# An encoder layer on one core: operands of wide products moved to byte 480 of a line of 512, and work beside the recurrence ordered anew

## The chip, the cores and the metric

The kernel runs on one core of a Trainium2 chip. Its time is the device time of one execution in microseconds (us). Engines are called as the profile calls them: PE (TensorE, with PEld for its weight loads), DVE (VectorE), ACT (ScalarE), POOL (GpSimd) and SP (SyncE, which issues the transfers). SBUF has 128 partitions; a tile lies at the same byte of each, and "byte 480 of a line of 512" means that this address, modulo 512, is 480.

## The reference

One layer of a bidirectional encoder, on two groups of 512 tokens with a model width of 1024 and shared weights, all in fp32:

```python
x = LN(alpha*x + 0.5*SwiGLU_1(x))                       # D_FF = 2816
h = x @ W_in                                            # MLA, RWKV-7 and gate columns
A = MLA(h_q, h_kv) @ P_mla                              # 8 heads
B = RWKV7_bidir(h_rwkv) @ P_rwkv                        # 8 heads of 64, both directions
x = LN(alpha*x + (sig(g_A)*A + sig(g_B)*B) @ W_o)
x = LN(alpha*x + CrossAttn(x, LN(mem)))                 # 4 heads of 128, 256 memory rows
x = LN(alpha*x + 0.5*SwiGLU_2(x))
```

The RWKV-7 part is a recurrence over the tokens: a state S of 64 x 64 per head is updated as S = S*w + (S a) b^T + v k^T and read as S r, once forward and once backward.

## The kernel before, in words

**Products.** Every fp32 matrix product is made of three products of rounded parts: high by high, high by low, low by high (`Bank.prod`, line 228; `Bank.mm` issues each at line 215). A "wide" product is one such matmul of 128 x 128 weights (the stationary operand) by 128 x 512 values (the moving operand). The weights are `whl` (high and low half in one tile); the moving operands are `xh` and `xl` (high and low parts of the activations, class `Acts`), `xo` (a streamed operand of a Strassen product, both parts in one tile), `mh` and `ml` (memory), `kp`, `cx`, `wd`, `ad`, `lw` and others in the projections and in MLA. There are 9344 of them with 512 columns.

**Weights.** `Stream.fetch` (line 136) has SP load a tile `wraw` of 128 x 1024, ACT cast it to the high half of `whl` (line 245), and an engine named by `Stream.low` subtract it for the low half (a "split", line 246 where that is POOL, 179 where it is DVE). `Stream.ahead` says how many tiles ahead of use this is done.

**Stages, in order of time.** FFN 1 (8 to 690 us) and FFN 2 (2056 to 2732) run as Strassen products of seven (`ffn`, `strassen`): a gate/up part (50 to 430 and 2056 to 2470), in which blocks of 36 products of `xh` and `xl` alternate with blocks of 48 of `xo`, and a down part (430 to 650 and 2470 to 2700) on `xo` alone. Between them: projections and MLA (690 to 1222), the recurrence (1222 to 1762), the last projections, W_o and cross attention (to 2055).

**The recurrence** (class `Recurrence`) handles four pairs of heads, called heads 0 to 3, one after another: `front` (products `bk` by `ar`), `inverse`, `chunks`. `inverse` inverts 32 x 32 triangular blocks: a loop of 30 steps on DVE (products `tm<-lw,dw`, then `dw<-dw,lw`, then `dw<-dw,tm`), transposes of `dw` to `xt` and `ct`, then 2 x 64 small matmuls, first of `xt` by `phi`, copied to `qt`, then of `ct` by `qt`, copied to `phi` (the "section"). `chunks` carries the state through eight chunks (`gs`, `uv`, `sn`). In the recurrence `Stream.low` is POOL and `Stream.ahead` 1.

**Work beside it.** A generator (`gate_work`, `memory_work`, `mla_work`) yields steps that do not depend on the recurrence. One step is one k-block: three wide products. `Recurrence.fill` takes steps at the place where it is called in the program, and the table `FILL` says how many each head takes in its front, in its loop (spread over 30 steps) and in its chunks.

**Order.** The program is written in one sequence, and a scheduler lists the instructions of each engine by it and by the waits between them. From the first product of `xt` on, and through the chunks, PE's order is pinned to the written one (`k.in_order`); `order` (line 195) adds such a dependency between two instructions of one engine without a wait.

**Addresses.** Pools on the left side of SBUF are stacked upward in the order in which they are opened, and pools on the right side downward from the top. Tiles of the right side (`whl`, some of the `Acts`) begin at byte 480 of a line of 512, since the top lies there; those of the left side begin wherever the sizes before them lead.

Of the kernel before, what the change touches and what calls it, by code (L numbers as in the profile page):

```python
# [11 lines left out]
F32 = mybir.dt.float32  # L12
# [45 lines left out]
PAUSE = 8  # L58
A_FILL = A_END - 16

FILL = ((72, 66, 30), (6, 50, 36), (8, 54, 36), (0, 38, 20))
STREAM_B = (
    tiles_of("w_ck", range(4), 8)
    + [("w_cv", k, n) for k in range(8) for n in range(4)]
# [713 lines left out]
def kernel(  # L778
# [79 lines left out]
    )  # L858


    rs = ExitStack()
    wp = ctx.enter_context(pool("w", "right"))
    x0 = ctx.enter_context(ExitStack())
# [52 lines left out]


    bp = ExitStack()
    bon = bp.enter_context(pool("bonus")).tile([P, HP, NC, G], F32, name="bon")
    with pool("p2") as sb:  # L920

        def tmp(tag, bufs):
# [170 lines left out]
        with pool("mla") as sm:  # L1093
# [8 lines left out]
            for h in range(HP):  # L1102
# [3 lines left out]
                for g in range(G):  # L1106
                    ks = shifted(proj(w, g), 3 + 3 * h)
                    b = aux()
                    b.prod(b.t, [((lw[0:64, 0, cols], lw[0:64, 1, cols]), (ad[0:64, 0, g], ad[0:64, 1, g]))])
                    ta = tmp("ta", 2)  # L1110
                    nc.scalar.activation(out=ta, in_=b.t, func=AF.Tanh, scale=0.5, bias=ha0[:, h : h + 1])
                    sq = tmp("sq", 2)
                    nc.scalar.activation(out=sq, in_=ks, func=AF.Square, scale=v("k_k", h))
                    b = Bank(k, "b")
                    for i in range(4):
                        b.mm(b.t[:, 2 * i : 2 * i + 2], sq[:, i * P : i * P + P], blk2)
                    m = sb.tile([P, 8], F32, name="kkn", tag="kkn", bufs=2)
                    nc.vector.tensor_scalar(out=m, in0=b.t[:, 0:8], scalar1=1e-24, scalar2=None, op0=ALU.max)
                    rstd_of(k, sb, m, "kk")
                    b = Bank(k, "b")  # L1120
                    mw = tmp("u", 1)
                    nc.vector.tensor_copy(mw.rearrange("p (a v) -> p a v", v=C), m.unsqueeze(2).to_broadcast([P, 8, C]))
                    for i in range(4):
                        b.tr(b.t[:, i * P : i * P + P], mw[:, i * P : i * P + P], k.ident)
                    nr = tmp("nr", 2)
                    nc.vector.scalar_tensor_tensor(
                        out=nr, in0=ks, scalar=nkk_c[:, h : h + 1], in1=b.t, op0=ALU.mult, op1=ALU.mult)
                    nc.sync.dma_start(out=d_rw[h][g][:, 1], in_=nr)
                    u = tmp("u", 1)
                    nc.gpsimd.tensor_scalar(  # L1130
                        out=u, in0=ta, scalar1=-1.0, scalar2=hka[:, h : h + 1], op0=ALU.add, op1=ALU.mult)
                    kn = tmp("kn", 2)
                    nc.vector.scalar_tensor_tensor(out=kn, in0=u, scalar=1.0, in1=ks, op0=ALU.add, op1=ALU.mult)
                    nc.sync.dma_start(out=d_rw[h][g][:, 3], in_=kn)
                    nc.gpsimd.tensor_scalar(out=ta, in0=ta, scalar1=-0.5, scalar2=-0.5, op0=ALU.mult, op1=ALU.add)
                    nc.gpsimd.tensor_tensor(out=ta, in0=ta, in1=nr, op=ALU.mult)
                    nc.sync.dma_start(out=d_rw[h][g][:, 2], in_=ta)
                    kp.append(kn)
                    attend(3)
# [86 lines left out]
    with pool("rw") as sb:  # L1226
# [4 lines left out]
        def early_rows():  # L1231
# [3 lines left out]
            for g in range(G):  # L1235
                ys.append(Acts(xpools[0], "x", 4, HP, "y"))
                rows(ys[g], [d_y[h][g] for h in range(HP - 1)])

        rec.memory = memory_norm(k, sb, mem, d_mt)
        for h, beside in enumerate(FILL):  # L1240
            rec.front(h, beside[0])
# [315 lines left out]
class Recurrence:  # L1557
# [106 lines left out]
    def inverse(self, h, beside):  # L1664
# [17 lines left out]
        dw = t4("dw")  # L1682
        nc.scalar.copy(dw, lw)
        lm, dm = lw.rearrange("p (i k) -> p i k", k=32), dw.rearrange("p (i k) -> p i k", k=32)
        for i in range(1, 31):
            if i < 30:
                tm = self.sb.tile([P, 256], F32, name="tm", tag="tm", bufs=2)
# [11 lines left out]
            if i < 30:  # L1699
                o = dm[:, i + 2 : 32, 0:i]  # L1700
                nc.vector.tensor_tensor(out=o, in0=o, in1=t, op=ALU.add)
        nc.vector.memset(dw[:, 0:1024:33], 1.0)
        xt, ct = t4("xt"), t4("ct")
        nc.vector.transpose(out=tj(xt), in_=dw.rearrange("p (t s) -> p s t", s=32))
# [3 lines left out]
        ra, rb = ([slice(64 * e + o, 64 * e + o + 32) for e in range(2)] for o in (0, 32))  # L1708

        k.in_order, k.pe_last = True, None  # L1710
        for j0, tag in ((0, "c"), (16, "b")):
            ps = [self.bank(tag) for _ in range(2)]
            for j in range(16):
                for e in range(2):
                    ps[e].mm(ps[e].t[rb[e], j * 32 : j * 32 + 32], phi[ra[e], e, j0 + j, 32:64], xt[ra[e], j0 + j])
            for e, cp in ((0, nc.scalar.copy), (1, nc.vector.tensor_copy)):
                cp(qt[rb[e], j0 : j0 + 16], ps[e].t[rb[e]].rearrange("p (j s) -> p j s", s=32))
        for j in (0, 16):
            for q in range(4):
                (nc.scalar.copy if q % 2 else nc.vector.tensor_copy)(diag(q, j), ct[32 * q : 32 * q + 32, j : j + 16])  # L1720
        for j0, tag in ((0, "c"), (16, "b")):
            ps = [self.bank(tag) for _ in range(2)]
            for j in range(16):
                for e in range(2):
                    ps[e].mm(ps[e].t[ra[e], j * 32 : j * 32 + 32], qt[rb[e], j0 + j], ct[rb[e], j0 + j])
            for e, cp in ((0, nc.scalar.copy), (1, nc.vector.tensor_copy)):
                cp(phi[ra[e], e, j0 : j0 + 16, 32:64], ps[e].t[ra[e]].rearrange("p (j s) -> p j s", s=32))
        k.in_order = False

    def chunks(self, h, beside, early_rows):  # L1730
# [260 lines left out]
```

## Time and profile before

| what | value |
|---|---|
| time, three runs | 2731.43, 2730.34, 2730.81 us; median 2730.81 |
| the profiled execution's own time | 2733.67 us |
| its span on the core | 2731.9 us |
| mean granted clock of PE | 0.968 |

PE is the busiest engine over the whole span. The page's second part shows the granted clock in 40 slices:

```profile
PE   8999999999999999997988887999999999999996
DVE  7888887999476888748474758656888888887987
PEclk9999999999999999998989898999999999999998
```

Each digit is a busy share in tenths, 9 being 90% or more, and for PEclk the clock that the throttle granted; a slice is 2731.9/40 = 68.3 us. Rows of windows give the start and end of the window and its length in us, then busy time and count of PE, PEld, DVE, ACT and POOL, the granted clock, the share of the DMA engines and GB/s. Rows of groups give line, engine, operation, output and inputs, shape and count, then busy us and the mean ns of one instruction, then the idle time before them and what ended it. Since matmuls are pipelined, the mean duration of one is longer than the distance from one start to the next; where PE has no idle, the distance is window length by count. Rows of the timeline give start and length in us. Rows of waits give the wait in all, how often, and the longest.

### The profile page before, as it was taken

What the parts mean: (1) busy time and instruction counts of PE and PEld (TensorE: products, weight loads), DVE (VectorE), ACT (ScalarE), POOL (GpSimd) and SP (SyncE); (2) the same over time, 40 slices, a digit from 0 to 9 for tenths busy, and PEclk for the clock granted to TensorE, in tenths of its full rate; (3) what the DMA queues carried; (4) which work ended last, traced back from release to release, by engine and by line L of the source; (5) the groups of instructions that cost most, each with busy time, mean ns of one, the idle gap of its engine ahead of it and who ended that gap; (6) DMA issues with size and microseconds to landing.
All of it is one profiled execution on the core that took longest, in us unless ns stands there. A gap on an engine that the chain in (4) does not pass through costs nothing. (4 is left out here: it accounts for less than half of the span.)

```text
span 2731.9 us, 40963 instructions
## 1 busy us (share of the span) xinstructions
PE 2576.3 (94%) x15344; PEld 2067.5 (76%) x15344; DVE 2098.0 (77%) x3742; ACT 1073.5 (39%) x1972; POOL 682.5 (25%) x465
## 2 busy tenths in 40 slices
PE   8999999999999999997988887999999999999996
PEld 7888887787767777776777666777787888887784
DVE  7888887999476888748474758656888888887987
ACT  5344332222453554554433432223544443342222
POOL 0233332442200001132123221102012323232443
PEclk9999999999999999998989898999999999999998
DMA  4344437671254433353434354451202443447751
GB/s 174 123 155 162 147 134 301 237 264 60 99 175 155 124 107 116 111 172 121 120 100 132 109 166 127 144 181 44 65 16 81 166 147 139 143 171 271 275 201 66
DMA packets 167143, 396.06 MB, mean 145 GB/s; under 512 B 41952, under 2 KB 52448, under 8 KB 166944
## 3 DMA queue, kind: packets, MB, share of 16 engines
q1 hardware_dynamic: 166944, 393.43, 41.8%
q8 instruction: 122, 2.00, 0.3%
q14 instruction: 77, 0.63, 0.1%
HBM read 259.41 MB, written 133.96 MB: 144 GB/s over the span
## 5 line engine op out<-in xcount | busy, mean ns | idle before, releaser
L215 PE MATMUL ps<-xo,whl 128*128 128x512 f32 x3792 | 896.9, 395 | 14.8 <-DVE z L179 9.1
L215 PE MATMUL ps<-xh,whl 128*128 128x512 f32 x2688 | 888.6, 402 | 15.3 <-ACT xh L245 12.9
L215 PEld LDWEIGHTS ps<-xo,whl 128*128 128x128 f32 x3792 | 712.9, 189 | 183.9 <-DVE z L179 6.9
L215 PEld LDWEIGHTS ps<-xh,whl 128*128 128x128 f32 x2688 | 509.3, 191 | 128.4 <-ACT xh L245 13.5
L215 PE MATMUL ps<-xl,whl 128*128 128x512 f32 x1344 | 536.2, 399 | 1.4 <-POOL xl L246 1.2
L245 ACT CAST whl<-wraw 128x512 fp32r<-128x512 f32 (+4 forms) x314 | 220.2, 712 | 296.3 <-PE ps L215 273.8
L179 DVE TENSOR_TENSOR whl<-wraw,whl 128x512 fp32r<-128x512 f32 (+4 forms) x269 | 277.4, 1042 | 59.5 <-ACT whl L245 59.2
L215 PEld LDWEIGHTS ps<-xl,whl 128*128 128x128 f32 x1344 | 256.4, 191 | 55.7 <-POOL xl L246 3.7
L684 POOL TENSOR_TENSOR s<-s,up 128x512 f32<-128x512 f32 x80 | 117.2, 1465 | 615.7 <-DVE up L179 394.8
L245 ACT CAST whl<-wt 128x512 fp32r<-128x512 f32 (+3 forms) x280 | 148.9, 557 | 270.3 <-PE ps L215 162.3
L179 DVE TENSOR_TENSOR whl<-wt,whl 128x512 fp32r<-128x512 f32 (+3 forms) x280 | 214.8, 788 | 13.5 <-ACT whl L245 13.5
L246 POOL TENSOR_TENSOR whl<-wraw,whl 128x1024 fp32r<-128x1024 f32 x45 | 108.8, 2419 | 364.8 <-ACT whl L245 321.3
L245 ACT CAST hop<-s 128x512 fp32r<-128x512 f32 x128 | 79.7, 623 | 244.7 <-POOL s L684 183.3
L179 DVE SCALAR_TENSOR_TENSOR x<-ps,x 128x512 f32<-128x512 f32 x184 | 124.6, 683 | 60.8 <-PE ps L215 57.1
L179 DVE TENSOR_TENSOR hop<-s,hop 128x512 fp32r<-128x512 f32 x128 | 121.1, 947 | 59.9 <-ACT hop L245 52.1
L246 POOL TENSOR_TENSOR xl<-x,xh 128x512 fp32r<-128x512 f32 x48 | 67.0, 1428 | 303.4 <-ACT xh L245 288.3
L179 DVE TENSOR_TENSOR wt<-wraw 128x512 f32<-128x512 f32 (+3 forms) x140 | 110.0, 787 | 1.3 <-DMA wraw<-in_wf_dram 0.2
L179 DVE TENSOR_TENSOR wt<-wraw,wt 128x512 f32<-128x512 f32 (+3 forms) x140 | 102.1, 730 | 5.5 <-DMA wraw<-in_wf_dram 3.5
L582 POOL TENSOR_TENSOR x<-x,s 128x512 f32<-128x512 f32 x48 | 70.2, 1467 | 129.0 <-DVE x L179 129.0
L179 DVE TENSOR_TENSOR p<-ps,p 128x512 f32<-128x512 f32 x120 | 82.3, 686 | 5.1 <-PE ps L215 1.5
L582 POOL TENSOR_TENSOR x<-x,z 128x512 f32<-128x512 f32 x48 | 71.2, 1484 | 52.7 <-DVE x L179 47.5
L215 PE MATMUL ps<-mh,whl 128*128 128x512 f32 x256 | 82.1, 398 | 1.0 <-ACT whl L245 1.0
(308 smaller groups left out, 3647.0 us busy)
## 6 DMA issues: line engine op xcount, KB each, us to landing
d_h<-hop SPq DMA_DIRECT2D x140, 512.0 KB, 2.6
xo<-d_h SPq DMA_DIRECT2D x140, 512.0 KB, 7.0
wraw<-in_wf_dram SPq DMA_DIRECT2D x95, 512.0 KB, 3.5
wraw<-in_wa_dram SPq DMA_DIRECT2D x57, 512.0 KB, 3.7
wraw<-in_wb_dram SPq DMA_DIRECT2D x32, 512.0 KB, 3.7
wraw<-in_wf_dram SPq DMA_DIRECT2D x36, 384.0 KB, 3.8
ld<-d_rw SPq DMA_DIRECT2D x24, 512.0 KB, 4.6
d_gate<-t SPq DMA_DIRECT2D x32, 256.0 KB, 2.3
```

The source lines that it names most:

```text
L179: inst = f(*args, **kw)
L215: self.last = order(k.tc, k.nc.tensor.matmul(out, a, b, start=start, stop=stop), self.last)
L245: nc.scalar.copy(hi, src)
L246: (low or nc.vector).tensor_tensor(out=lo, in0=src, in1=hi.bitcast(F32), op=ALU.subtract)
L582: eng.tensor_tensor(out=y[r, c], in0=y[r, c], in1=u, op=ALU.add)
L684: nc.gpsimd.tensor_tensor(out=s[:, i], in0=s[:, i], in1=up[:, i], op=ALU.mult)
```

## The change

1. **Gaps.** Three tiles that nothing reads or writes are added to left pools: 96 floats (384 bytes a partition) at the end of the constants, 64 floats (256 bytes) behind `bon`, 80 floats (320 bytes) in the pool `p2` of the projections. All that is allocated behind them moves up. By the addresses of the built program all operands of wide products then begin at byte 480 of a line of 512. Before, of the products with 512 columns, `xo` begins at byte 96 in 2976 and at 480 in 816, `xh` at 96 in 736 and at 480 in 1952, `xl` at 96 in 368 and at 480 in 976; `mh`, `ml` and the cross attention's `coh` and `col` at 96; `kp`, `cx`, `pt`, `wd` at 32; `ad` and `lw` at 352. 5264 products have an operand that moves: 1044 in FFN 1, 608 in projections and MLA, 768 between recurrence and FFN 2, 2844 in FFN 2.
2. **The recurrence.** `FILL` gets other numbers, and a table `BESIDE` takes steps behind each of the two groups of `xt` products and of the two of `ct` products in `inverse` (2, 4, 2 and 3 steps; 2 and 1 in the last head). During the loop of 30 steps `Stream.low` is DVE in place of POOL. Both copies of `qt` per group are on DVE (before, one on ACT and one on DVE), and DVE's copies of `ct` to `phi` are ordered behind the last of them. The number of wide products beside the recurrence is the same, 905 from the first front to the last chunk and its tail.

```diff
-FILL = ((72, 66, 30), (6, 50, 36), (8, 54, 36), (0, 38, 20))
+FILL = ((72, 46, 34), (8, 44, 30), (10, 44, 34), (0, 40, 16))
+BESIDE = ((2, 4, 2, 3),) * 3 + ((0, 2, 0, 1),)
...
+    cp.tile([P, 96], F32, name="gap")
...
-    bon = bp.enter_context(pool("bonus")).tile([P, HP, NC, G], F32, name="bon")
+    bonus = bp.enter_context(pool("bonus"))
+    bon = bonus.tile([P, HP, NC, G], F32, name="bon")
+    bonus.tile([P, 64], F32, name="gap")
...
+                    if h == g == 0:
+                        sb.tile([P, 80], F32, name="gap")
...
+        rec.weights = st
...
+        self.weights.low = nc.vector
         for i in range(1, 31):
...
+        self.weights.low = nc.gpsimd
...
-        for j0, tag in ((0, "c"), (16, "b")):
+        for n, (j0, tag) in enumerate(((0, "c"), (16, "b"))):
...
-            for e, cp in ((0, nc.scalar.copy), (1, nc.vector.tensor_copy)):
-                cp(qt[rb[e], j0 : j0 + 16], ps[e].t[rb[e]].rearrange("p (j s) -> p j s", s=32))
+            for e in range(2):
+                last = nc.vector.tensor_copy(
+                    qt[rb[e], j0 : j0 + 16], ps[e].t[rb[e]].rearrange("p (j s) -> p j s", s=32))
+            self.fill(BESIDE[h][n])
         for j in (0, 16):
             for q in range(4):
-                (nc.scalar.copy if q % 2 else nc.vector.tensor_copy)(diag(q, j), ct[32 * q : 32 * q + 32, j : j + 16])
+                to, src = diag(q, j), ct[32 * q : 32 * q + 32, j : j + 16]
+                if q % 2:
+                    nc.scalar.copy(to, src)
+                else:
+                    order(k.tc, nc.vector.tensor_copy(to, src), last)
...
+            self.fill(BESIDE[h][2 + n])
```

Three places show how the rows move. The first is PE in the section of head 1, from the last wide product of the loop to the first of the chunks (`uv`, `gs`). Before:

```order
L215 MATMUL ps<-xh_10971,whl 128x512
L215 MATMUL ps<-xt,phi 32x32 x64
L215 MATMUL ps<-ct,qt 32x32 x64
L215 MATMUL ps<-uv,phi 64x64 x8
L215 MATMUL ps<-gs,phi 64x64 x8
```

After, the second half of the `xt` products and the wide ones up to the first `ct` products:

```order
L217 MATMUL ps<-xt,phi 32x32 x32
L217 MATMUL ps<-xh_11144,whl 128x512
L217 MATMUL ps<-xl_11145,whl 128x512
L217 MATMUL ps<-xh_11144,whl 128x512 x2
L217 MATMUL ps<-xl_11145,whl 128x512
L217 MATMUL ps<-xh_11144,whl 128x512 x2
L217 MATMUL ps<-xl_11145,whl 128x512
L217 MATMUL ps<-xh_11144,whl 128x512
L217 MATMUL ps<-xh_11146,whl 128x512
L217 MATMUL ps<-xl_11147,whl 128x512
L217 MATMUL ps<-xh_11146,whl 128x512
L217 MATMUL ps<-ct,qt 32x32 x32
```

Twelve wide products stand there now; six stand behind the first half of the `xt` products, six behind the first half of the `ct` products and nine behind the second (by head: 30, 33, 33 and 9, before 6, 0, 0 and 0). From the last product of a front to the first `xt` product stand 75, 124, 98 and 107 wide products, before 110, 142, 127 and 102; in the chunks 72, 84, 69 and 48, before 85, 99, 75 and 54.

The second place is DVE in the middle of the loop of head 1. Before:

```order
L179 TENSOR_TENSOR tm<-lw,dw 128x225
L179 SCALAR_TENSOR_TENSOR dw<-dw,lw 128x15
L179 TENSOR_TENSOR dw<-dw,tm 128x15x15
L179 TENSOR_TENSOR tm<-lw,dw 128x224
L179 SCALAR_TENSOR_TENSOR dw<-dw,lw 128x16
```

After:

```order
L181 TENSOR_TENSOR tm<-lw,dw 128x225
L181 SCALAR_TENSOR_TENSOR dw<-dw,lw 128x15
L181 TENSOR_TENSOR whl<-wraw,whl 128x1024
L181 TENSOR_TENSOR dw<-dw,tm 128x15x15
L181 TENSOR_TENSOR tm<-lw,dw 128x224
```

A split has come in between two steps of the loop. With those just ahead of a loop, two, four, three and three stand there by head, of which one was on DVE before; in all 21 of the 45 splits that POOL had are DVE's.

The third place is DVE behind the loop of head 1. Before:

```order
L179 STREAM_TRANSPOSE ct<-dw 128x32x32
L179 COPY phi<-ct 32x16x32 x4
L179 COPY qt<-ps 32x512 x2
L179 COPY phi<-ps 32x16x32 x2
```

After:

```order
L181 STREAM_TRANSPOSE ct<-dw 128x32x32
L181 COPY qt<-ps 32x512 x4
L181 COPY phi<-ct 32x16x32 x4
L181 COPY phi<-ps 32x16x32 x2
```

The copies of `qt`, four in place of two, now come ahead of those from `ct` to `phi`.

More of the change, by code (lines that the diff above doesn't have):

```diff
@@ L1715, in inverse @@
                     ps[e].mm(ps[e].t[rb[e], j * 32 : j * 32 + 32], phi[ra[e], e, j0 + j, 32:64], xt[ra[e], j0 + j])
-            for e, cp in ((0, nc.scalar.copy), (1, nc.vector.tensor_copy)):
-                cp(qt[rb[e], j0 : j0 + 16], ps[e].t[rb[e]].rearrange("p (j s) -> p j s", s=32))
+            for e in range(2):
+                last = nc.vector.tensor_copy(
+                    qt[rb[e], j0 : j0 + 16], ps[e].t[rb[e]].rearrange("p (j s) -> p j s", s=32))
+            self.fill(BESIDE[h][n])
         for j in (0, 16):
             for q in range(4):
-                (nc.scalar.copy if q % 2 else nc.vector.tensor_copy)(diag(q, j), ct[32 * q : 32 * q + 32, j : j + 16])
-        for j0, tag in ((0, "c"), (16, "b")):
+                to, src = diag(q, j), ct[32 * q : 32 * q + 32, j : j + 16]
[3 more added lines that the diff above has]
+                    order(k.tc, nc.vector.tensor_copy(to, src), last)
+        for n, (j0, tag) in enumerate(((0, "c"), (16, "b"))):
             ps = [self.bank(tag) for _ in range(2)]
```

## Prediction

> **What bounds the kernel now.** I read the engine line of the page first, then its chain of waits by engine, then the busy time of each engine by stage, then, in the recurrence, the waits of PE and the timeline.
>
> ```profile
> span 2731.9 us, 40963 instructions
> PE 2576.3 (94%) x15344; PEld 2067.5 (76%) x15344; DVE 2098.0 (77%) x3742; ACT 1073.5 (39%) x1972; POOL 682.5 (25%) x465
> PE 32%; DVE 5%; ACT 2%; issue 1%; POOL 1%; DMA 1%; SPq 0%; POOLq 0%; ACTq 0%; DVEq 0%
> ```
>
> PE is busy for 94% of the span and leads the chain. The kernel can become faster in two ways only: the products themselves take less time, or the 156 us in which PE is idle shrink. The change tries the first in the wide stages and the second in the recurrence, so I cost them apart. The windows show where each is possible (columns: us from start, length, busy time and count of PE, PEld, DVE, ACT, POOL, then granted clock, DMA share, GB/s).
>
> ```profile
> 430.00:650.00 220.00, 212.21 (x913) 171.73 (x912) 196.19 (x289) 57.75 (x127) 85.77 (x60) 0.99 0.63 236
> 900.00:1222.00 322.00, 315.25 (x1590) 244.83 (x1590) 238.43 (x569) 168.78 (x332) 56.94 (x42) 0.99 0.39 122
> 1222.00:1795.00 573.00, 492.64 (x5913) 398.75 (x5910) 384.58 (x870) 213.15 (x386) 132.47 (x82) 0.89 0.42 132
> 1795.00:2055.00 260.00, 252.88 (x1276) 207.01 (x1275) 183.18 (x421) 106.67 (x215) 42.52 (x31) 1.00 0.20 66
> 2056.00:2470.00 414.00, 413.90 (x1780) 335.26 (x1781) 344.10 (x452) 164.09 (x287) 119.51 (x78) 1.00 0.42 150
> 2470.00:2700.00 230.00, 222.96 (x970) 178.24 (x969) 204.79 (x304) 55.72 (x123) 87.20 (x60) 0.99 0.55 204
> ```
>
> The gate/up part of the second FFN (2056 to 2470) has no idle at all on PE, the down parts 7 to 8 us. The recurrence with its tail (1222 to 1795) has 573.00 - 492.64 = 80 us of idle and the only low clock, 0.89.
>
> **Part 1: the gaps.** They add no instruction and move none; they move tiles by 384, 256 and 320 bytes a partition. By the addresses that the allocator gives, 5264 of the 9344 wide products (512 columns) then begin at byte 480 of a line of 512 with both operands: 1044 in FFN 1, 608 in the projections and MLA, 768 between the recurrence and FFN 2, 2844 in FFN 2. In FFN 1 `xh`, `xl` and one of the four streamed operands in `xo` are there already and the other three begin at byte 96; in FFN 2 all of them begin at 96. So the trace of before already holds the experiment: the same products at both bytes, in stages where PE never waits. Four windows that hold one kind each, then 17 repeats of both kinds together:
>
> ```profile
> 109.74:117.90 8.16, 8.16 (x38) 6.76 (x37) 7.18 (x10) 3.12 (x6) 2.27 (x2) 1.00 0.53 187
> 117.90:129.02 11.12, 11.12 (x50) 9.00 (x49) 9.57 (x14) 3.73 (x7) 2.27 (x2) 1.00 0.18 53
> 2115.04:2123.40 8.36, 8.36 (x37) 6.78 (x36) 6.10 (x9) 3.40 (x6) 3.97 (x3) 1.00 0.36 127
> 2123.40:2134.56 11.16, 11.16 (x49) 9.04 (x48) 10.72 (x14) 5.13 (x9) 3.80 (x3) 1.00 0.61 236
> 98.62:426.42 327.80, 327.80 (x1429) 268.00 (x1428) 281.33 (x365) 131.65 (x230) 104.47 (x69) 1.00 0.42 153
> 2115.04:2446.92 331.88, 331.88 (x1430) 269.03 (x1429) 283.52 (x366) 132.17 (x231) 106.20 (x69) 1.00 0.42 151
> ```
>
> The first holds 36 products of `xh` and `xl` in FFN 1, the second 48 of `xo`, the next two the same in FFN 2 (the counts are one or two higher because a product that straddles the edge counts in both). At byte 480: 8.16/36 = 226.7 ns. At byte 96: 8.36/36 = 232.2 ns for the same tiles and 11.16/48 = 232.5 ns for `xo`. The second window mixes 12 products at 480 with 36 at 96: 11.12 - 12 x 0.2267 = 8.40, 233.3 ns each. Clock 1.00 and no idle in all four, so neither throttle nor waits make the difference; the durations of single products agree, 389 and 394 ns:
>
> ```profile
> L215 PE MATMUL ps<-xh,whl 128*128 128x512 f32 x24 | 7.5, 389 | 0.0
> L215 PE MATMUL ps<-xh,whl 128*128 128x512 f32 x24 | 7.7, 394 | 0.0
> ```
>
> (the first of the window from 109.74, the second of that from 2115.04). FFN 1 and FFN 2 run the same code with the same engines beside it, and the difference holds over 17 repeats: 331.88 - 327.80 = 4.1 us for 17 x 48 products more at 96 is 5.0 ns each. If all come to 226.7, a block of 84 in FFN 2 saves 8.36 + 11.16 - 84 x 0.2267 = 0.48 us, 5.7 ns for each product, and in FFN 1 11.12 - 48 x 0.2267 = 0.24 us, 6.7 ns for each of the 36 that move; I take these, and 5.7 for the tail. FFN 1: 1044 x 6.7 = 7.0 us. FFN 2: 2844 x 5.7 = 16.2. Tail: 768 x 5.7 = 4.4. Projections and MLA: 608 products, many from bytes 32 and 352, for which no row gives a clean price: bounds 0 and 608 x 5.7 = 3.5, and I take the middle, 1.7. Sum 29.3.
>
> Does the gain reach the end? Where PE has no idle, all of it. In the down parts DVE is busy for 196.19 of 220 and 204.79 of 230 us, so PE could soon wait for it. There 324 products of FFN 1 and about 1060 of FFN 2 move, 2.2 + 6.0 = 8.2 us. The waits of PE there say how near that is:
>
> ```profile
> L215 PE MATMUL ps<-xo,whl 128*128 128x512 f32 x901 | 210.2, 394 | 7.8 <-DVE z L179 4.8 <-DVE x L179 1.7 <-DVE up L179 1.3
> L215 PE MATMUL ps<-xo,whl 128*128 128x512 f32 x922 | 220.6, 398 | 7.0 <-DVE z L179 4.3 <-DVE x L179 1.7 <-DVE up L179 1.1
> ```
>
> The first (FFN 1, some 580 of its products already at 480) waits 7.8 us, the second (all at 96) 7.0: the faster products brought 0.8 us more of waits. I take off 2 us; the bounds are 0 and 8.2. Part 1 is worth **27.3 us**.
>
> [...]
>
> **Part 2: the recurrence.** Each of four heads has a front, a loop of 30 steps on DVE (`dw`), a section of small products (`xt`, `ct`) and the chunks. Loops and sections of before, heads 0 to 3, in pairs:
>
> ```profile
> 1237.30:1274.40 37.10, 25.18 (x110) 20.50 (x111) 36.99 (x120) 12.27 (x17) 12.46 (x5) 0.89 0.42 134
> 1274.40:1286.10 11.70, 11.45 (x262) 8.93 (x262) 6.77 (x10) 7.06 (x12) 2.55 (x2) 0.50 0.26 71
> 1378.00:1413.50 35.50, 32.46 (x145) 26.59 (x146) 31.38 (x93) 10.78 (x15) 9.89 (x4) 1.00 0.32 102
> 1413.50:1425.70 12.20, 7.21 (x256) 6.94 (x257) 5.81 (x9) 7.86 (x13) 4.64 (x2) 0.50 0.30 87
> 1518.30:1554.50 36.20, 29.08 (x128) 23.73 (x127) 32.08 (x93) 11.60 (x16) 12.43 (x5) 0.93 0.34 102
> 1554.50:1564.70 10.20, 7.28 (x257) 7.04 (x257) 5.91 (x9) 5.80 (x10) 2.35 (x1) 0.50 0.15 39
> 1651.80:1685.90 34.10, 24.13 (x103) 18.83 (x103) 31.28 (x103) 6.51 (x9) 2.39 (x1) 0.91 0.44 142
> 1685.90:1693.80 7.90, 7.04 (x257) 6.91 (x257) 6.08 (x9) 4.74 (x9) 0.00 (x0) 0.50 0.49 158
> ```
>
> *Loops.* DVE sets their length, and POOL's splits sit inside: 5 + 4 + 5 + 1 = 15. One of them beside the steps, and what DVE pays for a split of its own in this stage:
>
> ```profile
> 1247.91 2.50 POOL L246 TENSOR_TENSOR whl<-wraw,whl 128x1024 fp32r<-128x1024 f32 x1 [3.04 <-ACT whl L245]
> 1248.09 2.35 DVE L179 SCALAR_TENSOR_TENSOR dw<-dw,lw 128x6 f32<-128x6 f32 x1
> 1250.82 0.21 DVE L179 SCALAR_TENSOR_TENSOR dw<-dw,lw 128x7 f32<-128x7 f32 x1
> L179 DVE TENSOR_TENSOR whl<-wraw,whl 128x1024 fp32r<-128x1024 f32 x2 | 2.4, 1222 | 0.4 <-ACT whl L245 0.4
> ```
>
> A step of 0.21 us takes 2.35 while POOL works: 15 x 2.14 = 32.1 us removed. The new order has 12 splits on DVE in the loops (two, four, three and three by head, those just ahead of a loop counted with it), where one stood before: 11 x 1.22 = 13.4 added. The loops become 18.7 us shorter. But 77 wide products leave them (404 between the last front product and the first of `xt`, 481 before), 77 x 0.227 = 17.5 us of cover. Idle in the four loops, 11.9 + 3.0 + 7.1 + 10.0 = 32.0, becomes 32.0 - 18.7 + 17.5 = 30.8: a gain of 1.2.
>
> *Waits in the sections.*
>
> ```profile
> PE ps L215 <- DVE xt L179: 30.7, 4, 11.9
> PE ps L215 <- ACT gs L1759: 9.2, 29, 1.1
> PE ps L215 <- ACT qt L1717: 6.6, 2, 4.3
> PE ps L215 <- ACT phi L1727: 2.2, 3, 0.9
> ```
>
> PE waits 6.6 + 2.2 = 8.8 us for `qt` and `phi`, the former because its copy on ACT stands behind copies and casts. Now both copies of `qt` are on DVE ahead of those of `phi`, and 6 to 12 wide products stand between: 8 us of it goes, at most 8.8. The wait for `xt`, 30.7 us, is the loops' idle of above and stays.
>
> *What the fills cost where they now stand.* The sections run at half the granted clock. What a wide product takes at that clock shows in another stretch; its window, two rows of its timeline (start, length), and the window behind the section of head 1:
>
> ```profile
> 1502.10:1508.70 6.60, 6.05 (x14) 4.38 (x15) 4.68 (x6) 6.19 (x11) 3.99 (x3) 0.50 0.76 259
> 1505.21 1.05 PE L215 MATMUL ps<-xh,whl 128*128 128x512 f32 x2
> 1506.49 1.05 PE L215 MATMUL ps<-xh,whl 128*128 128x512 f32 x2
> 1413.20:1433.70 20.50, 14.78 (x340) 13.20 (x342) 10.48 (x21) 9.51 (x15) 4.64 (x2) 0.50 0.39 98
> ```
>
> Three products in 1506.49 - 1505.21 = 1.28 us are 427 ns each, 200 more than at full clock. 99 more products stand in the sections (105 against 6): at most 99 x 0.200 = 19.8 us. Against it: after the section of head 1 the clock stays at 0.50 to 1433.70 (last row), 20.5 us with much idle in it; wide products keep PE full and may bring it back sooner, and then the chunks behind gain. I take +5, nearer the low end, because those last 8 us (14.78 - 7.21 = 7.6 busy, half of it lost to the clock) are there to be won back in each of four heads.
>
> [...]
>
> *The rest.* 40 wide products leave the chunks (273 of 313 stay), which wait 9.2 us for `gs` in 29 waits already: 40 x 0.227 = 9.1 us of cover, bounds 0 and +9; most of a chunk is still covered, +2. Ten more splits come to DVE from POOL outside the loops, most in and ahead of the fronts: 10 x 1.22 = 12.2 at most; PE has wide products in the fronts, +2. A new wait is possible: PE's order is pinned in a section, so a wide product whose `whl` is not split yet holds the `ct` products and all behind them, and DVE's copies of `phi` after these. One split of 2.50 us (row above) serves eight k-blocks, so a section of ten holds one or two: bounds 0 and 4 x 2.5 = +10, and I take 0, because the tile is fetched one ahead. Part 2: -1.2 - 8 + 5 + 2 + 2 = **-0.2 us**, bounds -15 (fills at -5, the rest at 0) and +42.
>
> **Sum.** 27.3 + 0.2 = 27.5 us off. The profiled execution took 2733.67 us with a span of 2731.9; the median of the runs is 2730.81. 2733.67 - 27.5 = 2706.2 for a profiled execution, 2730.81 - 27.5 = **2703.3** for the median.
>
> **Rivals.**
> A (forecast, 0.55): as above, 2703, from 2696 to 2711.
> B (0.18), the clock comes back inside the sections. For: fills are full-width work. Against: in head 0 a section with 11.45 of 11.70 us busy stayed at 0.50. Then +5 becomes about -5: 2693.
> C (0.15), the fills pay the half clock in full and the chunks lose their cover: +19.8 and +5 in place of +5 and +2: 2721.
> Partial (0.05): only one of the two operands' start counts and the tiles move together with something else: half of part 1, 2717.
> D (0.04), the start byte is not the cause (FFN 2's tiles differ from FFN 1's in more than the byte: other lines, other neighbours) and the change doesn't do what it says: 2731. Against: `xo` and `xh` differ inside FFN 1 itself, 233.3 against 226.7.
> E (0.03), slower: the chunks' fills, 40 of 313 fewer, no longer hold PE's activity up, and the clock stays low through them. PE work of 492.64 us at a clock of 0.89: each 0.01 costs 492.64/89 = 5.5 us. Part 1 is eaten from 0.84 on, and 0.83 gives 2736: 2730.8 - 27.5 + 6 x 5.5. For: PE is idle for 80 of 573 us there. Against: the work is the same, closer together.
>
> **Numbers.** Time 2703. The range takes in B and most of C, 2688 to 2719; the likeliest case's own is 2696 to 2711. About 0.2% (5.5 us) is what a measurement can tell from no change: faster 0.94 (A, B, C, partial, a bit of D), same 0.03, slower 0.03.
>
> **What would show it.** Blocks of `xo` and `xh` in both FFNs at 226.7 ns and 389 ns, the gate/up part of FFN 2 10 us shorter; if FFN 2 is still at 232, part 1 is wrong. `dw` steps of 2.35 us gone and no POOL split in the loops; the waits for `qt` and `phi` below 1 us; a granted clock of 1.00 before the end of a section says B, 0.50 throughout and longer waits for `gs` say C. In the down parts waits for `z` above 9 us would mean that DVE took part of the gain.

## The result, and the profile after

The changed kernel takes 2709.47 us (median of 4 runs, 2708.19 to 2711.83) against 2730.57 us before (median of 4, 2729.33 to 2731.43): a ratio of 0.9917, 95% interval 0.9904 to 0.993, that is 19 to 26 us less. The forecast was 2703, 27.5 us less. The profiled execution took 2711.83 us, its span 2710.0. From its page, the span and the engine line:

```profile
span 2710.0 us, 40977 instructions
PE 2548.4 (94%) x15344; PEld 2057.8 (76%) x15344; DVE 2104.9 (78%) x3769; ACT 1067.8 (39%) x1964; POOL 634.6 (23%) x446
```

PE is busy 28 us less with the same 15344 matmuls; its idle time has grown by 6 us (2731.9 - 2576.3 = 155.6 before, 161.6 now). Both traces hold every matmul, so the stages can be laid side by side by the start of the same matmul, counted in order of start (numbers 172, 1828, 2915, 5297, 11277, 12553, 14332 and the last mark the edges). Lengths in us, with the forecast of the change in each:

| stage | before | after | change | forecast |
|---|---|---|---|---|
| FFN 1 gate/up | 380.14 | 375.36 | -4.8 | 720 x 6.7 ns = -4.8 |
| FFN 1 down | 260.88 | 261.74 | +0.9 | 324 x 6.7 ns = -2.2 |
| projections, MLA | 523.69 | 521.74 | -2.0 | -1.7 |
| recurrence with its tail | 580.45 | 578.22 | -2.2 | -0.2 |
| last projections, W_o, cross attention | 261.26 | 258.41 | -2.9 | -4.4 |
| FFN 2 gate/up | 413.68 | 403.96 | -9.7 | 1780 x 5.7 ns = -10.1 |
| FFN 2 down | 242.46 | 240.78 | -1.7 | -6.0 |

(The forecast took 2 us off both down parts together. Matmul 172 starts at 50.0 us before and 50.7 after, so the changes sum to 22.4 and the last matmul starts 21.7 us earlier.) The gate/up parts came as forecast; the down parts gave 0.8 us of 8.2. The windows of the blocks that the prediction measured, now (columns as there: us from start, length, then busy time and count of PE, PEld, DVE, ACT, POOL, then granted clock, DMA share, GB/s):

```profile
109.59:117.75 8.16, 8.16 (x38) 6.76 (x36) 7.22 (x10) 3.06 (x6) 2.22 (x2) 1.00 0.52 184
117.75:128.63 10.88, 10.88 (x50) 9.01 (x48) 9.49 (x14) 3.77 (x7) 2.30 (x2) 1.00 0.17 57
2122.78:2130.94 8.16, 8.16 (x38) 6.76 (x36) 7.88 (x12) 2.40 (x5) 1.60 (x1) 1.00 0.43 154
2130.94:2141.82 10.88, 10.88 (x50) 9.01 (x48) 9.03 (x13) 4.42 (x8) 2.91 (x2) 1.00 0.24 81
```

In both FFNs 36 products of `xh` and `xl` take 8.16 us and 48 of `xo` 10.88: 226.7 ns everywhere, the value named. Then the down parts; first before, windows from the same matmul to the same matmul, FFN 1 and FFN 2:

```profile
430.20:691.00 260.80, 247.36 (x1088) 199.51 (x1086) 233.93 (x369) 69.52 (x143) 92.42 (x64) 0.98 0.57 210
2470.10:2712.60 242.50, 231.07 (x1013) 184.86 (x1011) 214.53 (x333) 56.21 (x124) 87.82 (x61) 0.99 0.52 194
```

and after:

```profile
426.00:687.80 261.80, 246.28 (x1089) 200.29 (x1087) 233.81 (x370) 69.44 (x143) 91.80 (x65) 0.97 0.57 210
2450.10:2690.90 240.80, 227.82 (x1013) 186.30 (x1011) 214.55 (x333) 55.98 (x123) 87.56 (x61) 0.98 0.53 196
```

The groups of the `xo` products after, in windows that start there and end at 647 and 2678 (the prediction showed those of before; `x`, `z` and `up` are sums that DVE makes of the products):

```profile
L217 PE MATMUL ps<-xo,whl 128*128 128x512 f32 x899 | 208.8, 394 | 10.1 <-DVE z L181 5.4 <-DVE x L181 3.2 <-DVE up L181 1.5
L217 PE MATMUL ps<-xo,whl 128*128 128x512 f32 x922 | 216.9, 395 | 8.5 <-DVE z L181 5.3 <-DVE x L181 1.7 <-DVE up L181 1.5
```

Two things are to be seen. PE's waits for DVE went from 7.8 to 10.1 and from 7.0 to 8.5 us. And PE's busy time itself fell by less than the price of the gate/up parts would have it: 1.1 us in FFN 1 and 3.3 in FFN 2, where 2.2 and 6.0 were counted. The price is not the reason. Matmuls 14347 to 14501 are 154 `xo` products of FFN 2's down part that follow one another without a break in both traces, first before, then after:

```profile
2475.71:2511.64 35.93, 35.93 (x155) 28.91 (x154) 27.50 (x45) 9.72 (x22) 7.73 (x7) 1.00 0.77 295
2455.76:2490.69 34.93, 34.93 (x156) 28.91 (x154) 27.50 (x45) 9.67 (x22) 7.25 (x7) 1.00 0.81 312
```

35.93/154 = 233.3 ns fell to 34.93/154 = 226.8, so the price was paid here too. What changed beside the waits is the clock behind one of them, a wait for `z`. The same products with the wait ahead of them, in FFN 1 before and after (matmuls 2721 to 2760), then in FFN 2 before and after (14669 to 14700):

```profile
641.05:653.95 12.90, 9.84 (x40) 7.74 (x39) 11.93 (x17) 2.86 (x7) 6.90 (x5) 0.87 0.01 2
636.94:651.18 14.24, 10.93 (x40) 8.50 (x39) 12.21 (x18) 4.07 (x7) 6.66 (x5) 0.76 0.04 8
2552.14:2560.91 8.77, 7.47 (x33) 5.74 (x31) 8.67 (x12) 1.41 (x3) 3.65 (x4) 1.00 1.01 408
2530.78:2541.72 10.94, 8.89 (x32) 6.89 (x31) 10.84 (x14) 2.33 (x5) 5.73 (x4) 0.84 1.00 383
```

The wait grew from 3.06 to 3.31 us and from 1.30 to 2.05 (length less busy time), and behind it PE was busy 1.1 and 1.4 us longer for the same products, at a granted clock of 0.76 in place of 0.87 and 0.84 in place of 1.00. A wait of this length doesn't always bring that: in the down part of FFN 1 of the same trace PE waits 2.04 us for `z` (up to 521.10) and keeps a clock of 1.00:

```profile
517.00:528.00 11.00, 8.96 (x40) 7.10 (x39) 10.90 (x16) 1.76 (x4) 4.40 (x4) 1.00 0.83 317
```

What decides it was not tried.

The recurrence. Loops and sections of heads 0 to 3 in pairs, then the whole with its tail, then PE's waits from 1200 to 1795:

```profile
1232.50:1264.10 31.60, 17.25 (x77) 13.99 (x78) 31.46 (x122) 9.36 (x13) 2.64 (x1) 0.84 0.24 75
1264.10:1280.80 16.70, 16.70 (x287) 13.13 (x287) 8.03 (x11) 7.14 (x13) 2.38 (x1) 0.69 0.30 86
1371.50:1403.90 32.40, 28.41 (x128) 23.23 (x129) 29.39 (x97) 12.76 (x17) 2.47 (x1) 1.00 0.36 122
1403.90:1421.20 17.30, 17.30 (x289) 13.61 (x289) 8.75 (x12) 6.91 (x11) 5.78 (x3) 0.70 0.20 52
1511.20:1542.40 31.20, 24.63 (x99) 19.31 (x98) 28.19 (x96) 10.69 (x15) 2.35 (x1) 0.92 0.30 101
1542.40:1557.50 15.10, 15.06 (x291) 11.90 (x291) 8.83 (x12) 5.87 (x9) 3.12 (x2) 0.83 0.26 68
1643.60:1677.20 33.60, 24.53 (x108) 19.92 (x107) 31.31 (x105) 7.54 (x10) 0.00 (x0) 0.90 0.48 162
1677.20:1686.80 9.60, 9.57 (x265) 8.08 (x265) 8.04 (x12) 3.77 (x7) 0.00 (x0) 0.64 0.53 161
1209.50:1787.70 578.20, 492.41 (x5980) 394.11 (x5981) 396.42 (x905) 215.10 (x388) 94.16 (x66) 0.91 0.42 135
```

```profile
PE ps L217 <- DVE xt L181: 31.9, 4, 14.3
PE ps L217 <- ACT gs L1779: 11.9, 29, 1.2
PE ps L222 <- DVE phi L181: 11.3, 15, 6.2
```

The loops are 142.9 - 128.8 = 14.1 us shorter, yet their idle went from 32.0 to 34.0. Of POOL's 15 splits three are left (POOL's x1 in the first three loops), each beside a step that it holds; steps of `dw` or `tm` over 2 us fell from 13 to 3. The sections have no idle left and no wait for `qt`; their clock rose from 0.50 to 0.69, 0.70, 0.83 and 0.64. A split on DVE in a loop costs what its row said; the second row is the step that POOL's last split still holds (timeline of head 1's loop, start and length):

```profile
1386.93 1.22 DVE L181 TENSOR_TENSOR whl<-wraw,whl 128x1024 fp32r<-128x1024 f32 x1
1398.51 2.36 DVE L181 SCALAR_TENSOR_TENSOR dw<-dw,lw 128x28 f32<-128x28 f32 x1
```

### The profile page after: what moved, and what is told of

It is laid out like the page before. It is cut to its first block, busy times and chain, and to the rows that moved or that the text cites. A ratio compares the mean times of both kernels' runs of the same rounds, so it can differ in the third digit from the quotient of the medians.

```text
span 2710.0 us, 40977 instructions
## 1 busy us (share of the span) xinstructions
PE 2548.4 (94%) x15344; PEld 2057.8 (76%) x15344; DVE 2104.9 (78%) x3769; ACT 1067.8 (39%) x1964; POOL 634.6 (23%) x446
## 4 chain that ended last, share of the span: by engine, by line
PE 53%; DVE 12%; ACT 3%; DMA 3%; issue 2%; POOL 1%; SPq 0%; POOLq 0%; ACTq 0%; DVEq 0%
PE ps L217 50%; PE ps L222 3%; DVE dw L181 2%; DVE whl L181 2%; DVE tm L181 1%; DVE z L181 1%; DVE rs L181 1%; DVE phi L181 1%; DVE x L181 1%; DMA ld<-d_rw 1%; ACT whl L247 1%; DVE wt L181 0%; POOL ln_z L359 0%; DVE gm L181 0%; DMA d_q<-st 0%
## 5 line engine op out<-in xcount | busy, mean ns | idle before, releaser
L217 PE MATMUL ps<-xo,whl 128*128 128x512 f32 x3792 | 882.2, 392 | 18.6 <-DVE z L181 10.6
L181 DVE TENSOR_TENSOR whl<-wraw,whl 128x512 fp32r<-128x512 f32 (+4 forms) x288 | 300.6, 1053 | 73.8 <-ACT whl L247 73.7
L181 DVE TENSOR_TENSOR whl<-wt,whl 128x512 fp32r<-128x512 f32 (+3 forms) x280 | 216.3, 794 | 14.5 <-ACT whl L247 14.5
L248 POOL TENSOR_TENSOR whl<-wraw,whl 128x1024 fp32r<-128x1024 f32 x26 | 63.7, 2448 | 367.4 <-ACT whl L247 300.6
```

The costliest lines, as they stand in the source:

```text
L181: inst = f(*args, **kw)
L217: self.last = order(k.tc, k.nc.tensor.matmul(out, a, b, start=start, stop=stop), self.last)
L248: (low or nc.vector).tensor_tensor(out=lo, in0=src, in1=hi.bitcast(F32), op=ALU.subtract)
```

## The experiments

### The two parts apart

The theory at this point: the two parts are independent; the gaps make products faster, and the recurrence moves little. First only the gaps (the three `gap` tiles added to the kernel before), then only the recurrence (the three taken out of the changed kernel).

```diff
+    cp.tile([P, 96], F32, name="gap")
...
+    bonus.tile([P, 64], F32, name="gap")
...
+                        sb.tile([P, 80], F32, name="gap")
```

> Part 1 alone: the kernel before with the three gaps, recurrence unchanged. Theory (the two parts are independent; the product count of the two traces gives 19.5 us to the stages outside the recurrence): 2711, the gate/up parts at 226.7 ns per wide product, the down parts of both FFNs together less than 2 us shorter. Rival (the gaps also move tiles of the recurrence, and part of the gain seen there is theirs): 2708 or less. Rival (a part of the gain outside needs the new recurrence): 2715 or more.

> Part 2 alone: the changed recurrence without the three gaps. Theory: the 2.2 us that the recurrence is shorter between the two traces, 2728.4, and every stage outside as before. Rival (the prediction's sum for part 2, -0.2): 2730.4. Rival (the half clock costs and only the gaps' faster products hide it): above 2732.

On the same chip, where the kernel before took 2734.25 us (median): the gaps alone 2715.97, a ratio of 0.9932 (0.9918 to 0.9945); the recurrence alone 2731.55, a ratio of 0.9987 (0.9978 to 0.9997). The gaps' ratio on the time of 2730.57 us gives 2712, next to the theory's 2711 (the time of 2715.97 belongs to a chip on which the kernel before is slower too). The product of the two ratios, 0.9919, agrees with the change's 0.9917, so nothing speaks against two independent parts. With the gaps alone the gate/up parts are 375.36 and 403.91 us, the down parts 261.40 and 241.87; the gain is in the gate/up parts. The recurrence alone gains 1 to 6 us by the times. By stage it can't be had from one trace: the stage from matmul 5297 to 11277 took 579.1 to 584.0 us in nine traces of kernels that share the old order (mean 581.0), and 578.2, 582.9 and 578.0 with the new one.

### Which start is fast

The gaps put both operands of a product at byte 480. Is 480 a good byte, 96 a bad one, or must the two operands agree? Five kernels move one side at a time.

The first changes the first gap of the gaps-only kernel, so that the left side begins at 256:

```diff
-    cp.tile([P, 96], F32, name="gap")
+    cp.tile([P, 40], F32, name="gap")
```

> The gaps of part 1 with 40 floats in place of 96 in the first: left-side operands begin at byte 256, the weights and the right side stay at 480. Theory (equal start of the two operands of a product is what is fast): a block of 84 products in FFN 2 takes 19.5 us as before or more, 2730 or more. Rival (byte 96 is a bad start and any other is good): 19.04 us, 2711. Rival (the start byte does not matter and the moved neighbourhood does): 2711 as well, with FFN 2 at 226.7 ns.

The second has no gap on the left and one on the right:

```diff
     wp = ctx.enter_context(pool("w", "right"))
+    wp.tile([P, 96], F32, name="gap")
```

> The kernel before with a gap of 384 bytes at the top of the right side instead: weights and all FFN operands begin at byte 96, the left side lies as before. Theory (equal start is fast, whatever the byte): a block of 84 takes 19.04 us in both FFNs, about 2711 to 2713. Rival (byte 480 itself is fast and 96 slow): 232.4 ns in FFN 1 too, 4.1 us more in its gate/up part, 2735 to 2750.

Both were as slow as before or slower: ratios of 1.0017 (1.0007 to 1.0027) and 1.0014 (1.0004 to 1.0025). At byte 256 a block of FFN 2 is still slow. Its 48 products of `xo`:

```profile
2121.91:2133.11 11.20, 11.20 (x50) 9.00 (x49) 9.96 (x13) 5.17 (x9) 3.68 (x3) 1.00 0.61 236
```

11.20/48 = 233.3 ns. At 96 it was 232.5 in this block of the kernel before and 233.3 in its FFN 1 and its down part, so 256 and 96 are not told apart. So 96 is not a bad byte among good ones, and the moved neighbourhood is not the cause. The second kernel did something else than its expectation says: the pool laid the gap below its three `whl` buffers, so that these stayed at 480 (6780 of the products) and only the `whl` of the other pool came to 96 (2004 products), while every FFN operand is at 96. One trace then has both kinds in one block of `xo`; first 11 products with weights at 96 (the last of `xh` and ten of `xo`), then 35 of `xo` with weights at 480:

```profile
119.05:121.54 2.49, 2.49 (x12) 2.06 (x11) 2.11 (x2) 0.87 (x2) 2.20 (x2) 1.00 0.30 54
122.00:130.13 8.13, 8.13 (x36) 6.59 (x35) 6.74 (x11) 2.80 (x5) 0.00 (x0) 1.00 0.13 50
```

2.49/11 = 226.4 ns against 8.13/35 = 232.3. The same moving operand is fast with weights at its own byte and slow with weights elsewhere. The test is a kernel in which all FFN operands and all weights are at 96, by a pool of its own that is opened first on the right:

```diff
+    ctx.enter_context(pool("edge", "right")).tile([P, 96], F32, name="gap")
     wp = ctx.enter_context(pool("w", "right"))
```

> One gap of 384 bytes on the right side alone, at the very top: every weight tile and every FFN operand begins at byte 96, none at 480; nothing on the left side moves. Theory (what is fast is that moving operand and weights begin at the same byte of 512, whatever that byte is; in the kernel with both at 96 in part, products with weights at 96 were 227 ns apart and those with weights left at 480 232): blocks of 48 and of 36 at 226.7 ns in both FFNs, gate/up parts as with the three gaps, about 2714 to 2717 on the chip where these took 2716. Rival (byte 480 itself is fast): 232.4 ns in both FFNs, 2737 or more.

```profile
2115.97:2126.85 10.88, 10.88 (x49) 9.01 (x48) 10.40 (x14) 5.79 (x11) 4.39 (x3) 1.00 0.62 242
```

10.88/48 = 226.7 ns in FFN 2, gate/up parts of 375.36 and 403.96 us, and 2716.09 us, a ratio of 0.9927 (0.9903 to 0.9951) to the kernel before, as with the three gaps (0.9932). One gap does the work of three, and byte 480 has no merit of its own. The last two kernels ask how exactly the two must agree: 32 bytes apart (first gap of 88 floats), and 256 apart (32 floats).

> The gaps with 88 floats in place of 96 in the first: left-side operands begin at byte 448, 32 bytes from the weights' 480. Theory (equal start within 512 bytes): slow, 231 to 234 ns in FFN 2. Rival (only the position within 64 bytes counts for neighbours, or anything near is near enough): 226.7 ns.

> The gaps with 32 floats in the first: left-side operands begin at byte 224, 256 bytes from the weights' 480. Theory (the start must be equal modulo 512): 232 to 234 ns in FFN 2. Rival (equal modulo 256 is enough): 226.7 ns, and 2712 to 2717 in all.

The blocks of 48 of FFN 2, the first at 448, the second at 224:

```profile
2121.14:2132.34 11.20, 11.20 (x49) 9.02 (x48) 10.86 (x14) 5.19 (x9) 3.66 (x3) 1.00 0.62 235
```

```profile
2116.20:2127.08 10.88, 10.88 (x49) 9.01 (x48) 10.42 (x12) 5.75 (x11) 4.38 (x3) 1.00 0.64 242
```

32 bytes apart is slow (233.3 ns; one run, 2733.1 us), 256 apart is fast (226.7 ns; one run, 2716.41 us). Agreement modulo 256 was enough, against the theory, which wanted 512; of what was tried, 0 and 256 bytes apart were fast, and 32, 128 and 224 slow. Other distances were not tried.

### Where the gain of the down parts went

In the down parts I suspected DVE's load, as the prediction did. This pair takes a large piece of it away: in the down parts the low half of the weights of `FfnWeights.op` is copied on ACT in place of DVE's subtraction. The high half is then not subtracted from it, so less is computed.

```diff
-    def op(self, src):
+    def op(self, src, down):
...
-        split(self.k.nc, hi, lo, src)
+        if down:
+            self.k.nc.scalar.copy(hi, src)
+            self.k.nc.scalar.copy(lo, src)
+        else:
+            split(self.k.nc, hi, lo, src)
...
-                yield self.op(get(b))
+                yield self.op(get(b), n >= 2 * NP)
```

> The kernel before, in whose down parts the low half of the Strassen weights is a plain copy on ACT in place of DVE's subtraction (the subtraction of the high half is left out there); it takes some 60 x 0.78 + 40 x 0.95 us of work from DVE in each FFN. Theory (DVE sets the pace of the down parts): each gets 5 us or more shorter, PE's waits there fall, 2720 or less. Rival (the waits come from the chain from one Strassen sum to the next, not from DVE's load): within 3 us of before.

> The same edit on the kernel with the three gaps. Theory (DVE's load ate the gain of the faster products in the down parts): against the kernel without gaps and with the same edit the down parts now gain the 8.2 us of the prediction, so the whole gains about 26 us where the gaps alone gained 18. Rival (the chain of Strassen sums or a delay of PE itself ate it): the gain stays at about 18, with at most 2 us in the down parts.

Without gaps 2717.61 us, a ratio of 0.9944 (0.9919 to 0.9969); with them 2696.87, 0.9862 (0.9835 to 0.989). The down parts, FFN 1 and FFN 2, first without gaps, then with them:

```profile
431.20:686.50 255.30, 246.51 (x1088) 199.93 (x1087) 161.71 (x268) 109.72 (x250) 89.16 (x66) 0.98 0.60 216
2467.70:2703.30 235.60, 227.89 (x1012) 184.15 (x1011) 140.91 (x228) 94.19 (x226) 83.10 (x61) 1.00 0.55 198
```

```profile
426.50:679.70 253.20, 243.89 (x1088) 199.81 (x1087) 162.60 (x268) 109.55 (x250) 89.04 (x66) 0.98 0.61 219
2443.60:2676.20 232.60, 223.91 (x1013) 184.29 (x1011) 142.05 (x230) 94.79 (x229) 82.93 (x61) 0.99 0.57 208
```

With DVE at 162 and 141 us in place of 234 and 215, the parts are 5.5 and 6.9 us shorter without any gap: DVE's load does set their pace. And the gaps now bring 2.1 and 3.0 us there, 5.1 in all, where they brought 0.8 beside the loaded DVE. The whole gains 20.7 us with the gaps, between the theory's 26 and the rival's 18. That settles most of it, not all: FFN 1 gains what was forecast (2.2), FFN 2 half (3.0 of 6.0). By the starts of its `xo` products, those less than 0.3 us apart went from 232.4 to 226.9 ns (912 and 910 of them), which is the full price; what of it did not reach the end went into longer breaks between products (1.6 us among the `xo` products, 0.9 among the others).

The same relief with nothing left out: in the changed kernel, one of the seven splits of each down step goes to POOL.

```diff
-        split(self.k.nc, hi, lo, src)
+        split(self.k.nc, hi, lo, src, low)
...
-                yield self.op(get(b))
+                yield self.op(get(b), nc.gpsimd if n >= 2 * NP and b == "B22" else None)
```

> The changed kernel with one of seven splits of each down step (that of B22) on POOL in place of DVE, 15 per FFN. Theory (DVE's load is the pace of the down parts, so any relief counts): some 14 us of DVE work leave each down part; with 87 us away 5.5 to 7 us were gained, so 1 to 3 us each here, a ratio to before of about 0.990. Rival (a split on POOL holds DVE's own two-input work as in the loops of the recurrence, and POOL's sums x come late): 2 to 10 us slower than the changed kernel.

2706.0 us, a ratio of 0.9906 (0.989 to 0.9923). Against the changed kernel's 0.9917 the intervals overlap, so by the times it is not told apart. By stage the down parts are 257.64 and 237.61 us, 4.1 and 3.2 less than in the changed kernel, and the waits ahead of the `xo` products fell from 10.1 to 7.3 us and from 8.5 to 6.5.

### What the recurrence's edits are worth one by one

After the change the clock in the sections was up, and I took rival B for shown: the wide products in the sections bring the clock back and pay. The next kernel takes them out again, with the old table, and leaves the other edits.

```diff
-FILL = ((72, 46, 34), (8, 44, 30), (10, 44, 34), (0, 40, 16))
-BESIDE = ((2, 4, 2, 3),) * 3 + ((0, 2, 0, 1),)
+FILL = ((72, 66, 30), (6, 50, 36), (8, 54, 36), (0, 38, 20))
+BESIDE = ((0, 0, 0, 0),) * 4
```

> The changed kernel with the old table FILL and nothing in BESIDE: no wide products inside the sections; splits of the loops on DVE and both copies of qt on DVE stay. Theory (the wide products in the sections bring the clock back, rival B of the prediction): the four sections are at 0.50 to their ends again, the granted clock over the recurrence and its tail falls from 0.91 to 0.89, and the recurrence is 4 to 8 us longer than in the changed kernel, a ratio to before of 0.9935 to 0.995. Rival (the forecast: they cost the half clock, +5): faster than the changed kernel by 3 to 6 us, 0.990. In both, the loops have 77 wide products more, and PE waits for xt less than the 31.9 us of the changed kernel.

2695.03 us, a ratio of 0.9861 (0.9846 to 0.9875): faster than both kernels, some 15 us below the change (0.9861/0.9917 = 0.9944), and further from my theory than its rival was. Loops and sections in pairs, and the whole:

```profile
1229.80:1261.60 31.80, 25.18 (x109) 19.86 (x109) 31.72 (x124) 13.26 (x18) 1.88 (x1) 0.97 0.39 112
1261.60:1275.60 14.00, 10.36 (x262) 8.45 (x262) 9.62 (x14) 7.79 (x14) 5.53 (x5) 0.50 0.68 218
1367.80:1401.30 33.50, 32.41 (x142) 26.51 (x143) 29.38 (x97) 12.61 (x17) 2.39 (x1) 1.00 0.38 114
1401.30:1408.80 7.50, 6.37 (x257) 6.01 (x257) 7.21 (x9) 5.23 (x9) 1.57 (x1) 0.62 0.21 74
1502.10:1533.80 31.70, 29.54 (x128) 23.79 (x128) 28.51 (x98) 12.69 (x17) 1.14 (x1) 1.00 0.38 115
1533.80:1541.60 7.80, 6.40 (x257) 5.92 (x257) 7.44 (x11) 3.68 (x7) 1.23 (x1) 0.66 0.41 110
1625.50:1658.40 32.90, 22.93 (x99) 18.33 (x100) 30.09 (x104) 6.41 (x9) 0.00 (x0) 0.91 0.42 136
1658.40:1666.10 7.70, 7.06 (x257) 6.97 (x258) 6.93 (x11) 3.73 (x7) 0.00 (x0) 0.50 0.51 174
1208.50:1768.70 560.20, 489.08 (x5980) 393.28 (x5981) 395.80 (x910) 214.68 (x388) 79.38 (x61) 0.91 0.45 139
```

From PE's waits there:

```profile
PE ps L217 <- DVE xt L181: 12.6, 4, 9.6
```

Read against the changed kernel: the loops are as short (129.9 us, 128.8 there), but PE is busy in them for 110.1 us and not 94.8, because the old table leaves the wide products where DVE's steps leave PE nothing else. The wait for `xt` is 12.6 us and not 31.9, and that for `phi` (11.3 us there, one of 6.2 at the front of head 2) is 5.1. The sections take 37.0 us in place of 58.7. Heads 0 and 3 are at 0.50 in all of theirs, as the theory said, and head 1 from 1403.10, 1.80 us after the start of its section, past its end (0.50 from there to 1416.80); head 2's mean of 0.66 was not taken apart. But the granted clock over the whole is 0.91 in both: the sections' better clock bought nothing in the end. The recurrence is 560.2 us, 18.0 less than in the changed kernel and 20.8 less than the mean of 581.0 of the old order.

The last kernel undoes the other half, the splits:

```diff
-        self.weights.low = nc.vector
```

> The changed kernel with the splits of the loops back on POOL. Theory (a split on POOL holds DVE's steps): steps of 2.35 us are back, the loops get 10 to 18 us longer in all (forecast: 18.7) and nothing covers it, since the loops have fewer wide products: 10 us or more slower than the changed kernel, 0.9955 or more. Rival (PE has cover enough, or a split on DVE costs the loop as much as one on POOL): within 4 us of the changed kernel.

2718.11 us, a ratio of 0.995 (0.9933 to 0.9966) against the change's 0.9917: slower by about 9 us by the times, 3.8 in the recurrence's stage of the one trace (582.0). The loops, with POOL's splits in them again:

```profile
1230.90:1263.70 32.80, 18.39 (x83) 14.94 (x85) 32.69 (x120) 9.01 (x13) 7.41 (x3) 0.83 0.22 72
1371.80:1408.00 36.20, 28.40 (x128) 23.23 (x129) 32.08 (x93) 12.50 (x17) 12.24 (x5) 0.93 0.35 110
1514.30:1548.30 34.00, 21.96 (x96) 17.85 (x96) 29.88 (x93) 10.56 (x15) 9.59 (x4) 0.87 0.31 93
1648.80:1682.80 34.00, 25.08 (x108) 19.74 (x108) 31.16 (x103) 7.55 (x10) 4.81 (x2) 0.95 0.51 167
```

They sum to 137.0 us, 8.2 more than in the changed kernel, and PE's idle in them to 43.2, 9.2 more. Both numbers lie just below what the theory asked for (10 to 18), and above the rival's 4. That the trace shows only 3.8 us of it at the end of the stage fits its scatter of 5 us; it is not explained further.

## Why the prediction was right, and where it was not

**What bounds the kernel.** Right: the gain came from shorter products in stages where PE has no idle. Of the 21.7 us between the two traces 14.5 are in the two gate/up parts.

**Part 1, the price per product.** The blocks came to 226.7 ns and the gate/up parts moved by 4.8 and 9.7 us, forecast 4.8 and 10.1. It could be read off before, because FFN 1 and FFN 2 held the same products at both bytes. What the prediction made of it, "byte 480", was only half read: in that trace the weights were at 480 in every one of those windows, so "at 480" and "at the weights' byte" could not be told apart. The kernel with everything at 96 told them apart.

**Part 1, the way to the end.** This is the step that failed, "I take off 2 us" for the down parts. The change brought 0.8 us of 8.2 there, so 7.4 should have come off. That alone is 5.4 us of the 6.4 by which the forecast was too good (27.5 against 21.1). The prediction named DVE's pace, saw the sign of it (7.8 us of waits with some fast products, 7.0 without), and sized it from those 0.8 us, where the bound at 8.2 was the better choice: PE's waits ahead of the `xo` products grew by 2.3 and 1.5 us, and with DVE relieved the gaps bring 5.1 us. What it did not have at all is the clock: behind the longer waits for `z` PE was busy 1.1 and 1.4 us longer for the same products. Together these are 6.3 of the 7.4 us; the rest is not traced. The price was not at fault, since back-to-back products of FFN 2's down part went from 233.3 to 226.8 ns. The sign that the prediction had named, waits for `z` above 9 us, did not come (5.4 and 5.3 us), though DVE took the gain.

**Part 1, the rest.** The tail gave 2.9 us of 4.4; over all traces with and without moved operands there it is 2.3 (mean 259.0 against 261.3 us). Projections and MLA gave 2.0 for 1.7, but that stage took 521.4 to 523.8 us in three traces with the same addresses there, and over all traces the difference is about 1. Of the 608 products that it counted there, 344 had nothing to gain, a reason that the prediction could have had: by the addresses of the built programs `kp` and `qp`, `pt` and `vhl`, `ad` and `lw` began at equal bytes before too. Consecutive products of `kp` by `qp` (those less than 0.3 us apart) were 234.3 ns apart before and after, so there an equal start did not bring 226.7; what limits them was not tried.

**Part 2.** The sum, -0.2, is within what can be seen (1.3 by the stage means, 1 to 6 us by the times of the recurrence alone). Its two halves had the right signs and were each a few us too large; that the small sum came out is in part luck, since the errors of 3.9 and 6.5 us largely cancel. Splits on DVE and `qt` on DVE alone, by the prediction's terms -18.7 - 8 + 2 = -24.7, measured -20.8 (the kernel without products in the sections). The new tables, forecast 17.5 + 5 + 2 = +24.5, measured +18.0. In the first half the loops fell by 14.1 us and not 18.7; the term let all 15 of POOL's splits go, and three stayed. So a gain of 21 us stood in the change and was given back by the other half of it, and the prediction shows why: 77 wide products left the loops, where PE waits for DVE in any case.

**The rivals.** B was half true: the clock did come back inside the sections (0.70 over head 1's, 0.50 before), but taking these products out again made the kernel faster (2695.03 us): the clock came back and the gain did not. Nor did it come back at once: the four sections, with PE busy in 58.63 of their 58.70 us, had 0.64 to 0.83, and head 1's, with PE busy in all of its 17.30 us, was at 0.51 over its first 10, at 0.88 over the next 2.10 and at 1.00 over the last 5.20. C did not come: the chunks' waits for `gs` grew from 9.2 to 11.9 us, not more. The partial rival and D fell with the kernel that has both operands at 96: neither byte 480 nor one operand alone makes the difference. E did not come: the granted clock rose from 0.89 to 0.91.

## What to carry to other kernels

When the same instruction stands in two stages with two durations, the trace already holds the experiment; but vary both operands before naming the cause. Here, in the FFNs, products were 226.7 ns apart where the moving operand and the weights began at the same byte or 256 bytes apart, and 232.3 to 233.3 ns where they began 32, 128 or 224 bytes apart; one unused tile of 384 bytes was enough to arrange the first. The gain in the price of a product reached the end where PE had no idle (14.5 us of 14.9 in the gate/up parts) and hardly where PE waited for DVE (0.8 of 8.2 in the down parts), so take it stage by stage, and ask in each what the engine that is next would do and what a longer wait would do to the clock. When an edit has a gain and a cost of the same size, run the half without the cost: here it was 15 us better than the whole.

## What the runs showed of the hardware

- In the FFNs, back-to-back products of 128 x 128 by 128 x 512 at full clock were 226.7 ns apart when moving operand and weights began 0 or 256 bytes apart (both at 480, both at 96, 224 with 480), and 232.3 to 233.3 ns when they were 32, 128 or 224 bytes apart (448, 96 and 256 with 480): 2.5 to 2.9%. In these runs the distance between products went with where the two operands begin relative to each other. What the mechanism is, no run shows.
- One block of 48 with weights that change from one byte to the other changes its rate within it, 226.4 to 232.3 ns, so it is a matter of each product's pair and not of the stage.
- A split of 128 x 1024 on POOL held a DVE step of 0.21 us for 2.35; the same split on DVE took 1.22. In these loops it was cheaper on DVE, the engine that sets their length: with the splits back on POOL they took 137.0 us in place of 128.8.
- A wait of 2.05 us on PE in FFN 2's down part was followed by a granted clock of 0.84 over the 10.94 us from the matmul before it, where a wait of 1.30 us at the same place in the kernel before left it at 1.00; in FFN 1's down part of the same trace a wait of 2.04 us left it at 1.00 too.
